# Down projections cut in half between the gate and up groups of a gated feed-forward

## The chip, the core and the metric

The kernel runs on one core of one Trainium2 chip. The metric is the device time of one execution in microseconds (us). Five engines of the core work side by side, each through its own queue in order: TensorE (PE: matmuls; PEld are its weight loads), VectorE (DVE), ScalarE (ACT), GpSimd (POOL) and SyncE (SP, which here issues DMAs only).

## The reference

Two decoder layers over 512 tokens of width 1024 in float32, each a mixer and then a gated feed-forward with a causal convolution of width 3 on its gate. Only the feed-forward is touched by the change:

```
def gated_conv_ffn(x, w_gate, w_up, conv_w, conv_b, w_down):
    g = jnp.einsum('bsd,df->bsf', x, w_gate)          # 1024 -> 2816
    g = causal_dwconv3(g, conv_w) + conv_b
    up = jnp.einsum('bsd,df->bsf', x, w_up)
    return jnp.einsum('bsf,fd->bsd', jax.nn.silu(g) * up, w_down)   # 2816 -> 1024

for layer in range(2):
    h = h + mixer(rms_norm(h, norm_mix[layer]))
    h = h + gated_conv_ffn(rms_norm(h, norm_ffn[layer]), ...)
return rms_norm(h, final_norm)
```

## The kernel before

**Precision by parts.** Every operand of a matmul is held as two tiles, a rounded part (`hi`) and the remainder (`lo`), and every product is three matmuls: hi by hi, hi by lo, lo by hi (`mm3`, L152). So each weight tile and each activation tile needs one ScalarE copy (the `hi`) and one VectorE subtraction (the `lo`). `parts` (L145) does this for weights, `split` (L257) for activations. `summed` (L136) makes the `lo` in another way: ScalarE writes the negated weight, and an accumulating DMA that POOL issues adds the weight to it.

**Groups.** The 2816 hidden channels are 22 rows of 128 (`NF`). `Ffn.hidden(f)` (L757) makes rows f and f+1, gate and up: a group. Groups 0 and 2 use plain matmuls (`direct`, L592). Groups 4 to 20 use `both` (L681), a fast scheme of block products: seven products each for gate and up, 14 in all, each of four inner blocks by three matmuls of 256 columns. They run in the order g1 u1 g5 g6 u5 u6 g2 g7 u2 u7 g4 g3 u4 u3. For their weights VectorE first forms sums of blocks (`s12`, `s34`), and ScalarE and VectorE split those. The names in the profile are `whi_a11`, `whi_s12g`, `wlo_g` and so on for gate, with u for up, and `g_8a` or `u_8b` for the PSUM banks.

**After the products.** ScalarE and VectorE bring the products together out of PSUM into `rows` (gate) and `kept` (up), run the convolution (`c`, `conv`, L561: one ScalarE and two VectorE steps), the silu (`s`, L570) and the product with up. Then `act` (L575) splits the two rows into the four buffers of `acts` (`a_hi`, `a_lo`), and the second buffer pair of a group is the last to be ready.

**Down parts.** `PARTS` (L516) says which rows of the down projection stand behind which groups: rows 0 and 1 behind groups 0 and 2, rows 2 to 5 behind group 4, rows 6 to 9 behind groups 6 and 8, and so on by four; the last part (18 to 21) stands behind groups 18 and 20:

```
PARTS = (((0, 2), 0, 2), ((4,), 2, 6), ((6, 8), 6, 10), ((10, 12), 10, 14),
         ((14, 16), 14, 18), ((18, 20), 18, 22))
for groups, a, b in PARTS:
    for f in groups:
        ffn.hidden(f)
    ...
    project(f"d0_{a}", w_ffn_down[0], ffn.acts, list(range(a, b)), nxt)
```

Part (6, 10) therefore uses rows of both groups before it, one of which has just ended. With four `acts` buffers, the rows of the next group can be split only as these are read for the last time.

In layer 0 a part is a call of `project` (L286), with 1024 output columns in two halves of 512; one half is four PSUM banks, and VectorE adds each to the residual `h`. In layer 1 the tokens are the rows of the output instead (`lhs` is the activation, `rhs` the weight), and a part is a call of `down` (L1145) with eight pieces of 128 tokens by 512 columns that are added to `y`. Its weights are fetched a row of 128 by 1024 at a time. The last part of layer 1 also does the final norm, for which `fin`, the gain, is fetched into one of the staging tiles.

**What is shared.** Weights are fetched by SP into four staging tiles (`raw`, L129) and split into six pairs of buffers (`whi`, `wlo`, L138 and L146). Groups and down parts draw on the same staging tiles, buffers and the seven PSUM banks of `ps_mm`. A scheduler sets the order of the instructions on each engine from the program order and its own account of the times; where the program says `inorder` or `behind`, it is bound to that.

Of the kernel before, what the change touches and what calls it, by code (L numbers as in the profile page):

```python
# [20 lines left out]
FF = 2816  # L21
NF = FF // P
# [10 lines left out]
def tile_trunk(ctx: ExitStack, tc: tile.TileContext, x, norm_mix, norm_ffn, final_norm,  # L33
# [3 lines left out]
    nc = tc.nc  # L37
# [4 lines left out]
    wp = ctx.enter_context(tc.tile_pool(name="wp", bufs=1))  # L42
# [26 lines left out]
    small = cp.tile([P, LINE], F32, name="small")  # L69
# [20 lines left out]
    eps = small[:, 1:2]  # L90
# [42 lines left out]
    def weights(src, a, b, name):  # L133
        return parts(*fetch(src, a, b, name))
# [54 lines left out]
    class Norm:  # L189
# [93 lines left out]
        turn[0] += 1  # L283
        return padded[turn[0] % NPADDED]

    def project(name, w, acts, ks, norm, before=None):  # L286

        for gi in range(2):
            c0 = gi * 512
            chunks = {}  # L290
            for i in range(0, len(ks), 2):
                k0 = min(ks[i], ks[i + 1])
                hi, lo = weights(
                    w[k0 * P : (k0 + 2) * P, c0 : c0 + 512].rearrange("(k p) c -> p k c", p=P),
                    2, 512, f"{name}_{gi}_{k0}")
                chunks[k0], chunks[k0 + 1] = (hi, lo, 0), (hi, lo, 1)
# [12 lines left out]
            group(f"{name}{gi}", range(4), ks, lhs, lambda k, j: acts[k], 4, done,  # L309
                  before if gi == 0 else None)  # L310
# [37 lines left out]
    def mixer0():  # L348
        nonlocal prm0
        w = w_in_even[0]  # L350
        with tc.tile_pool(name="m0", bufs=1) as mp:
# [152 lines left out]
            def b_done(j, ps):  # L504
# [8 lines left out]

    PARTS = (((0, 2), 0, 2), ((4,), 2, 6), ((6, 8), 6, 10), ((10, 12), 10, 14),  # L516
             ((14, 16), 14, 18), ((18, 20), 18, 22))
    HALF = S // 2
    NP = NK // 2
    PAIRS = [k for i in range(NP) for k in (i, i + NP)]  # L520
# [25 lines left out]
    class Ffn:  # L546
# [45 lines left out]
        def direct(self, f, normed, sets, ch, before=lambda i, j: None):  # L592

            layer = self.layer
            banks = {}
            for js in sets:
                for i, k in enumerate(PAIRS):
                    for j in js:
                        before(i, j)
                        hi, lo = ch["gu"[j // 2], i // 4]  # L600
                        c = slice((j % 2) * P, (j % 2 + 1) * P)
                        if j not in banks:
                            banks[j] = mm_bank(f"gu{layer}_{f}_{j}")
                        mm3(banks[j], (hi[:, i % 4, c], lo[:, i % 4, c]), hg_k(k),
                            i == 0, i == NK - 1)

            def evacuate():
                r = self.r
                gates = []
                for j in range(2):  # L610
                    t = padded_tile()
                    if normed:
                        nc.scalar.copy(t[:, 2:], banks[j])
                    else:
                        nc.vector.tensor_tensor(t[:, 2:], banks[j], r, ALU.mult)
                    s = self.silu(self.conv(t, f + j), f + j)
                    if not normed:
                        nc.gpsimd.tensor_tensor(s, s, r, ALU.mult)
                    gates.append(s)
                for j, s in enumerate(gates):  # L620
                    nc.vector.tensor_tensor(s, banks[2 + j], s, ALU.mult)
                    self.act(f + j, s)

            return evacuate

# [55 lines left out]
        def both(self, f):  # L681

            layer, ap, n = self.layer, self.ap, f"{self.layer}_{f}"
# [6 lines left out]
            w = self.unit(f"a11_{n}")  # L690
# [3 lines left out]
            for key in "gu":  # L694
# [6 lines left out]
                w = self.unit(f"s12{key}_{n}")  # L701
# [18 lines left out]
            lo, hi = slice(2, 2 + HALF), slice(2 + HALF, 2 + S)  # L720
# [4 lines left out]
            s, pending = {}, {}  # L725
# [23 lines left out]
                    s[0] = self.silu(self.conv(pads[0], f), f)  # L749
            nc.vector.tensor_tensor(s[1][:, HALF:], kept[:, 2, :], s[1][:, HALF:], ALU.mult)  # L750
            nc.vector.tensor_tensor(s[1][:, :HALF], pending["u", 4], s[1][:, :HALF], ALU.mult)  # L751
            self.act(f + 1, s[1])
            s0 = s[0].rearrange("p (a b) -> p a b", a=2)
            nc.vector.tensor_tensor(s0, kept[:, :2, :], s0, ALU.mult)
            self.act(f, s[0])

        def hidden(self, f, before=lambda i, j: None):  # L757
            if f == 0:
                def first(i, j):
                    before(i, j)  # L760
# [10 lines left out]
                rest()  # L771
            elif f == 2:
                self.direct(2, True, ((0, 1), (2, 3)), self.ch)()
            else:
                self.both(f)

    def ffn0(norm):
        nonlocal prm1
        with tc.tile_pool(name="f0", bufs=1) as ap:
            def sums(kp):  # L780
                return [ap.tile([P, 2, HALF], F32R, name=f"t23{i}_{kp}") for i in "hl"]

            ffn = Ffn(0, prm0, norm, ap, sums)
            nxt = None
            for groups, a, b in PARTS:
                for f in groups:
                    ffn.hidden(f)
                if b == NF:
                    prm1 = params1()
                    nxt = Norm("m1", lambda k: prm1("mix", k))  # L790
                project(f"d0_{a}", w_ffn_down[0], ffn.acts, list(range(a, b)), nxt)
            return nxt


# [264 lines left out]
    def ffn1(norm):  # L1059
        with tc.tile_pool(name="f1", bufs=1) as ap:  # L1060
# [4 lines left out]
            ffn = Ffn(1, prm1, norm, ap, sums)  # L1065
            acts = ffn.acts
# [11 lines left out]
                if i < 2:  # L1078
                    turn_residual(j, i)

            for groups, a, b in PARTS:
                for f in groups:
                    ffn.hidden(f, before=before)
                last = b == NF
                if last:
                    fin = wp.tile([P, D], F32, tag="raw", bufs=4, name="fin")
                    nc.scalar.dma_start(
                        fin, final_norm.rearrange("(o d) -> o d", o=1).to_broadcast([P, D]))
                    root = small[:, 2:3]
                    nc.scalar.activation(root, eps, AF.Sqrt)  # L1090
# [15 lines left out]
                def done(piece, ps):  # L1106
                    t, c0, c1 = piece
                    dst = y[t][:, c0:c1]
                    nc.vector.tensor_tensor(dst, ps, dst, ALU.add)  # L1109
                    if not last:  # L1110
                        return
# [29 lines left out]
                if last:  # L1141
                    pieces[-1:] = [(NT - 1, 512, 768), (NT - 1, 768, D)]
# [45 lines left out]
```

## Time and profile before

| | |
|---|---|
| median of 3 runs | 994.29 us (994.14 to 994.36) |
| the profiled execution, its own time | 994.15 us |
| its span in the trace | 992.4 us |
| granted clock of TensorE, mean | 0.998 |
| regular pair of groups with its down part | 62.19 to 62.28 us |
| DMA | 125.07 MB, mean 126 GB/s |

The profile is of one execution, and times in it are counted from the start of its span. A row of the stretches gives length and busy time of each engine; a row of the timeline gives start, duration, engine, source line, operation and tiles, and in brackets how long the engine was idle before it and what ended the wait. A matmul's duration holds its way through the array, which overlaps the next one; the pace is the distance between starts. The chain of work that ended last is followed back from the end through what each piece waited for. Stretches in which TensorE runs from one matmul to the next show idle time of the other engines that costs nothing.

### The profile page before, as it was taken

What the parts mean: (1) busy time and instruction counts of PE and PEld (TensorE: products, weight loads), DVE (VectorE), ACT (ScalarE), POOL (GpSimd) and SP (SyncE); (2) the same over time, 40 slices, a digit from 0 to 9 for tenths busy, and PEclk for the clock granted to TensorE, in tenths of its full rate; (3) what the DMA queues carried; (4) which work ended last, traced back from release to release, by engine and by line L of the source; (5) the groups of instructions that cost most, each with busy time, mean ns of one, the idle gap of its engine ahead of it and who ended that gap; (6) DMA issues with size and microseconds to landing.
All of it is one profiled execution on the core that took longest, in us unless ns stands there. A gap on an engine that the chain in (4) does not pass through costs nothing.

```text
span 992.4 us, 14934 instructions
## 1 busy us (share of the span) xinstructions
PE 982.9 (99%) x5905; PEld 875.6 (88%) x5905; DVE 728.5 (73%) x1104; ACT 536.3 (54%) x806; POOL 105.3 (11%) x121
## 2 busy tenths in 40 slices
PE   9999999999999999999999999999999999999997
PEld 6788888898999989999888988888989899898996
DVE  6897458967785877858988665399668768687676
ACT  5623346744653746537668634675546366363664
POOL 2141031200000000000300001211000010000100
PEclk9999999999999999999999999999999999999999
DMA  7442225544553645536423513435546456464542
GB/s 246 133 146 85 86 88 131 121 148 118 133 147 97 181 121 132 148 98 180 136 87 93 182 54 97 105 91 130 143 101 159 124 125 173 94 163 126 123 112 85
DMA packets 83073, 125.07 MB, mean 126 GB/s; under 512 B 4308, under 2 KB 56252, under 8 KB 83004
## 3 DMA queue, kind: packets, MB, share of 16 engines
q1 hardware_dynamic: 74028, 98.24, 31.4%
q0 software_dynamic: 7056, 23.60, 13.3%
q10 hardware_dynamic: 1920, 2.30, 0.7%
q8 instruction: 46, 0.75, 0.3%
q14 instruction: 23, 0.19, 0.1%
HBM read 98.42 MB, written 2.10 MB: 101 GB/s over the span
## 4 chain that ended last, share of the span: by engine, by line
PE 94%; issue 1%; DVE 1%; DMA 1%; ACT 0%; DVEq 0%; POOLq 0%; ACTq 0%
PE d L154 4%; PE d L153 4%; PE d L155 4%; PE dn L153 4%; PE dn L154 4%; PE dn L155 4%; PE gu L153 3%; PE gu L154 3%; PE gu L155 3%; PE v L153 1%; PE oo L155 1%; PE oo L153 1%; PE v L155 1%; PE oe L155 1%; PE oe L154 1%; PE v L154 1%
## 5 line engine op out<-in xcount | busy, mean ns | idle before, releaser
L153 PE MATMUL dn<-whi_dn,a_hi 128*128 128x512 f32 (+1 forms) x180 | 69.4, 386 | 0.0
L154 PE MATMUL dn<-wlo_dn,a_hi 128*128 128x512 f32 (+1 forms) x180 | 69.3, 385 | 0.0
L154 PE MATMUL d<-a_lo,whi_d 128*128 128x512 f32 x176 | 68.7, 390 | 0.0
L155 PE MATMUL d<-a_hi,wlo_d 128*128 128x512 f32 x176 | 68.5, 389 | 0.0
L155 PE MATMUL dn<-whi_dn,a_lo 128*128 128x512 f32 (+1 forms) x180 | 67.9, 385 | 0.0
L153 PE MATMUL d<-a_hi,whi_d 128*128 128x512 f32 x176 | 66.9, 390 | 0.0
L566 DVE SCALAR_TENSOR_TENSOR c<-rows,prm,c 128x512 f32<-128x512 f32 x88 | 66.4, 766 | 0.0
L141 POOL DMA_DIRECT2D wlo_g<-raw_g x22 | 19.1, 867 | 373.9 <-ACT wlo_g L140 257.9
L1109 DVE TENSOR_TENSOR y<-dn,y 128x512 f32<-128x512 f32 (+1 forms) x49 | 32.5, 674 | 23.3 <-PE dn L155 23.0
L140 ACT ACTIVATE wlo_g<-raw_g 128x1024 fp32r<-128x1024 f32 x22 | 23.2, 1056 | 42.4 <-PE dn L154 42.4
L572 ACT ACTIVATE s<-c,prm 128x512 f32<-128x512 f32 x44 | 31.7, 720 | 20.5 <-DVE c L566 20.4
L679 DVE TENSOR_TENSOR wlo_s34u<-s34u,whi_s34u 128x1024 fp32r<-128x1024 f32 x18 | 22.0, 1225 | 27.9 <-ACT whi_s34u L678 27.9
L155 PEld LDWEIGHTS dn<-whi_dn,a_lo 128*128 128x128 f32 x180 | 33.8, 188 | 7.3 <-DVE a_lo L262 0.2
L678 ACT ACTIVATE whi_s12u<-s12u 128x1024 fp32r<-128x1024 f32 x18 | 18.9, 1051 | 39.3 <-PE d L154 33.7
L153 PEld LDWEIGHTS dn<-whi_dn,a_hi 128*128 128x128 f32 x180 | 33.8, 188 | 7.0 <-ACT a_hi L260 0.2
L154 PEld LDWEIGHTS dn<-wlo_dn,a_hi 128*128 128x128 f32 x180 | 33.8, 188 | 6.4
L154 PEld LDWEIGHTS d<-a_lo,whi_d 128*128 128x128 f32 x176 | 33.1, 188 | 7.3 <-DVE a_lo L262 0.2
L305 DVE TENSOR_TENSOR h<-d,h 128x512 f32<-128x512 f32 x48 | 32.5, 683 | 9.2 <-PE d L155 9.2
L153 PEld LDWEIGHTS d<-a_hi,whi_d 128*128 128x128 f32 x176 | 32.8, 188 | 7.0
L155 PEld LDWEIGHTS d<-a_hi,wlo_d 128*128 128x128 f32 x176 | 33.0, 188 | 6.7
L260 ACT ACTIVATE a_hi<-s 128x512 fp32r<-128x512 f32 x44 | 27.6, 628 | 16.1 <-DVE s L751 7.4
L149 DVE TENSOR_TENSOR wlo_dn<-raw_dn,whi_dn 128x1024 fp32r<-128x1024 f32 x22 | 26.8, 1220 | 11.6 <-ACT whi_dn L148 11.6
(1274 smaller groups left out, 3469.1 us busy)
## 6 DMA issues: line engine op xcount, KB each, us to landing
raw_g<-in_w_ffn_gate_dram SPq DMA_DIRECT2D x36, 512.0 KB, 4.6
raw_u<-in_w_ffn_up_dram SPq DMA_DIRECT2D x36, 512.0 KB, 4.7
wlo_g<-raw_g POOLq DMA_DIRECT2D x22, 512.0 KB, 4.7
raw_d<-in_w_ffn_down_dram SPq DMA_DIRECT2D x22, 512.0 KB, 4.0
raw_dn<-in_w_ffn_down_dram SPq DMA_DIRECT2D x22, 512.0 KB, 4.0
wlo_u<-raw_u POOLq DMA_DIRECT2D x19, 512.0 KB, 4.6
raw_oe<-in_w_out_even_dram SPq DMA_DIRECT2D x8, 512.0 KB, 3.6
raw_g<-in_w_ffn_gate_dram SPq DMA_DIRECT2D x16, 256.0 KB, 2.9
```

Source lines behind the costliest of these rows:

```text
L140: first = nc.scalar.activation(lo, raw, AF.Copy, scale=-1.0)
L141: nc.gpsimd.dma_start(lo, raw, accum_op=ALU.add)
L149: behind(nc.vector.tensor_tensor(lo, raw, hi.bitcast(F32), ALU.subtract), after[0])
L153: nc.tensor.matmul(ps, lhs[0], rhs[0], start=start, stop=False)
L154: nc.tensor.matmul(ps, lhs[0], rhs[1], start=False, stop=False)
L155: nc.tensor.matmul(ps, lhs[1], rhs[0], start=False, stop=stop)
L260: nc.scalar.activation(hi, src, AF.Copy, scale=scale)
L305: nc.vector.tensor_tensor(h[k], ps, h[k], ALU.add)
L566: nc.vector.scalar_tensor_tensor(c, t[:, i : S + i], prm("cf", i * NF + ft), c, op0=ALU.mult, op1=ALU.add)
L572: nc.scalar.activation(s, c, AF.Silu, bias=self.prm("bf", ft))
L679: nc.vector.tensor_tensor(lo, src, hi.bitcast(F32), ALU.subtract)
L1109: nc.vector.tensor_tensor(dst, ps, dst, ALU.add)
```

## The change

The whole part behind each pair of groups becomes two halves of 512 columns, one behind each group. Columns 0 to 511 of part (6, 10) follow group 8, as before; columns 512 to 1023 follow group 10. Parts (2, 6), (10, 14) and (14, 18) go the same way, behind groups 4 and 6, 12 and 14, 16 and 18. Part (0, 2), with both halves behind group 2, and part (18, 22), behind group 20, stay whole. Behind the first group of each pair (6, 10, 14, 18) the splits of its two rows stand after the half, since the buffers are still read there. In layer 1 all parts but the last now go through `group`, with weights in tiles of two rows by 512 columns.

```
+    STEPS = [(0, False, []), (2, False, [(0, 2, 0), (0, 2, 1)]), (4, False, [(2, 6, 0)])]
+    for f in range(6, NF - 2, 4):
+        STEPS += [(f, True, [(f - 4, f, 1)]), (f + 2, False, [(f, f + 4, 0)])]
+    STEPS[-1][2].append((NF - 4, NF, 1))
```

`half_weights` is the loop that `project` had for its weights, for one half; `project` takes the halves it is to do:

```
+    def project(name, w, acts, ks, norm, before=None, halves=(0, 1)):
+        for gi in halves:
+            chunks = half_weights(name, w, ks, gi)
```

`hidden` returns the function that does the splits, in place of doing them:

```
-                    self.act(f + j, s)
+                return [(f + j, s) for j, s in enumerate(gates)]
...
-            self.act(f + 1, s[1])
...
-            self.act(f, s[0])
+            return [(f + 1, s[1]), (f, s[0])]
...
+            def split_acts():
+                for ft, row in rows:
+                    self.act(ft, row)
+            return split_acts
```

The loop of layer 0:

```
-            for groups, a, b in PARTS:
-                for f in groups:
-                    ffn.hidden(f)
...
-                project(f"d0_{a}", w_ffn_down[0], ffn.acts, list(range(a, b)), nxt)
+            for f, late, down_parts in STEPS:
+                acts = ffn.hidden(f)
+                if not late:
+                    acts()
+                for a, b, half in down_parts:
...
+                    project(f"d0_{a}", w_ffn_down[0], ffn.acts, list(range(a, b)), nxt,
+                            halves=(half,))
+                if late:
+                    acts()
```

And of layer 1, where the body of the old loop is kept as `last_down` for the last part:

```
+            def half_down(a, b, half):
+                ks, cs = list(range(a, b)), slice(half * 512, half * 512 + 512)
+                chunks = half_weights(f"dn{a}", w_ffn_down[1], ks, half)
...
+                group(f"dn{a}_{half}", range(NT), ks, lhs, rhs, 4,
+                      lambda t, ps: add(y[t][:, cs], ps, t))
...
+            for f, late, down_parts in STEPS:
+                splits = ffn.hidden(f, before=before)
+                if not late:
+                    splits()
+                if f == NF - 2:
+                    last_down(NF - 4, NF)
+                    break
+                for part in down_parts:
+                    half_down(*part)
+                if late:
+                    splits()
```

More of the change, by code (lines that the diff above doesn't have):

```diff
@@ L284, in padded_tile, with half_weights @@
         return padded[turn[0] % NPADDED]
[L286 to L296, printed above, removed]
+    def half_weights(name, w, ks, gi):
+        chunks = {}
+        for i in range(0, len(ks), 2):
+            k0 = min(ks[i], ks[i + 1])
+            hi, lo = weights(
+                w[k0 * P : (k0 + 2) * P, gi * 512 : gi * 512 + 512]
+                .rearrange("(k p) c -> p k c", p=P), 2, 512, f"{name}_{gi}_{k0}")
+            chunks[k0], chunks[k0 + 1] = (hi, lo, 0), (hi, lo, 1)
+        return chunks
+    def project(name, w, acts, ks, norm, before=None, halves=(0, 1)):
+        for gi in halves:
+            chunks = half_weights(name, w, ks, gi)
             def lhs(k, j):
@@ L512, in mixer0 @@
             return nxt
-    PARTS = (((0, 2), 0, 2), ((4,), 2, 6), ((6, 8), 6, 10), ((10, 12), 10, 14),
-             ((14, 16), 14, 18), ((18, 20), 18, 22))
+    STEPS = [(0, False, []), (2, False, [(0, 2, 0), (0, 2, 1)]), (4, False, [(2, 6, 0)])]
+    for f in range(6, NF - 2, 4):
+        STEPS += [(f, True, [(f - 4, f, 1)]), (f + 2, False, [(f, f + 4, 0)])]
+    STEPS[-1][2].append((NF - 4, NF, 1))
     HALF = S // 2
@@ L770, in hidden @@
                     self.normalize(kp)
-                rest()
+                rows = rest()
             elif f == 2:
-                self.direct(2, True, ((0, 1), (2, 3)), self.ch)()
+                rows = self.direct(2, True, ((0, 1), (2, 3)), self.ch)()
             else:
-                self.both(f)
+                rows = self.both(f)
+            def split_acts():
+                for ft, row in rows:
+                    self.act(ft, row)
+            return split_acts
     def ffn0(norm):
@@ L784, in ffn0 @@
             nxt = None
-            for groups, a, b in PARTS:
-                for f in groups:
-                    ffn.hidden(f)
-                if b == NF:
-                    prm1 = params1()
-                    nxt = Norm("m1", lambda k: prm1("mix", k))
-                project(f"d0_{a}", w_ffn_down[0], ffn.acts, list(range(a, b)), nxt)
+            for f, late, down_parts in STEPS:
[3 more added lines that the diff above has]
+                for a, b, half in down_parts:
+                    if b == NF and half == 0:
+                        prm1 = params1()
+                        nxt = Norm("m1", lambda k: prm1("mix", k))
+                    project(f"d0_{a}", w_ffn_down[0], ffn.acts, list(range(a, b)), nxt,
+                            halves=(half,))
+                if late:
+                    acts()
             return nxt
@@ L1079, in before, with add, lhs, rhs @@
                     turn_residual(j, i)
[L1081 to L1090, printed above, removed]
+            def add(dst, ps, t):
+                nc.vector.tensor_tensor(dst, ps, dst, ALU.add)
+            def half_down(a, b, half):
+                ks, cs = list(range(a, b)), slice(half * 512, half * 512 + 512)
+                chunks = half_weights(f"dn{a}", w_ffn_down[1], ks, half)
+                def lhs(k, t):
+                    ts_ = slice(t * P, (t + 1) * P)
+                    return acts[k][0][:, ts_], acts[k][1][:, ts_]
+                def rhs(k, t):
+                    hi, lo, n = chunks[k]
+                    return hi[:, n, :], lo[:, n, :]
+                group(f"dn{a}_{half}", range(NT), ks, lhs, rhs, 4,
+                      lambda t, ps: add(y[t][:, cs], ps, t))
+            def last_down(a, b):
+                fin = wp.tile([P, D], F32, tag="raw", bufs=4, name="fin")
+                nc.scalar.dma_start(
+                    fin, final_norm.rearrange("(o d) -> o d", o=1).to_broadcast([P, D]))
+                root = small[:, 2:3]
+                nc.scalar.activation(root, eps, AF.Sqrt)
                 ch = {}
@@ L1108, in done @@
                     dst = y[t][:, c0:c1]
-                    nc.vector.tensor_tensor(dst, ps, dst, ALU.add)
-                    if not last:
-                        return
+                    add(dst, ps, t)
                     sq = tp.tile([P, S], F32, tag="sq", name=f"sqf{t}_{c0}")[:, : c1 - c0]
@@ L1140, in ffn1 @@
                 pieces = [(t, c, c + 512) for t in range(NT) for c in (0, 512)]
-                if last:
-                    pieces[-1:] = [(NT - 1, 512, 768), (NT - 1, 768, D)]
+                pieces[-1:] = [(NT - 1, 512, 768), (NT - 1, 768, D)]
                 down(f"dn{a}", list(range(a, b)), pieces, lhs, rhs, done)
+            for f, late, down_parts in STEPS:
[9 more added lines that the diff above has]
+                    splits()
     def down(name, ks, pieces, lhs, rhs, on_done):
```

## The prediction

> **What bounds the kernel now.** The page comes first: shares of busy time, and the chain that ended last.
>
> ```profile
> span 992.4 us, 14934 instructions
> PE 982.9 (99%) x5905; PEld 875.6 (88%) x5905; DVE 728.5 (73%) x1104; ACT 536.3 (54%) x806; POOL 105.3 (11%) x121
> ...
> PE 94%; issue 1%; DVE 1%; DMA 1%; ACT 0%; DVEq 0%; POOLq 0%; ACTq 0%
> ```
>
> TensorE (PE) is busy in 99% of the span, and the chain is PE's own work for 94%. A change that moves work without removing any can then win only PE's pauses. Next, the busy times by stretch show where those are: one pair of groups with its down part (14 and 16 of layer 0, cut into second group, part, next group), a whole pair, and the end.
>
> ```profile
> 326.47:346.60 20.13, 20.13 (x169) 20.10 (x169) 15.39 (x24) 14.34 (x24) 0.86 (x1) 1.00 0.63 176
> 346.60:368.40 21.80, 21.80 (x98) 17.89 (x98) 18.02 (x29) 7.94 (x10) 0.86 (x1) 1.00 0.51 141
> ...
> 388.67:450.87 62.20, 62.20 (x434) 58.27 (x434) 46.09 (x71) 33.65 (x51) 3.44 (x4) 1.00 0.51 136
> 942.24:963.36 21.12, 20.31 (x169) 20.06 (x168) 15.34 (x24) 14.17 (x23) 0.86 (x1) 1.00 0.51 137
> 985.70:992.40 6.70, 0.00 (x0) 0.00 (x0) 2.16 (x9) 1.30 (x4) 0.00 (x0) 0.68 0.20 78
> ```
>
> Columns: stretch, length, busy time of PE, PEld, VectorE (DVE), ScalarE (ACT) and POOL, granted clock, DMA share, GB/s. In the regular part PE is never idle, and DVE has room in both kinds of stretch (15.4 of 20.1, 18.0 of 21.8). One stretch differs: the last group of layer 1 takes 21.12 us, 0.81 of it idle.
>
> PE's starts give the pace. 256-column matmuls follow each other at 0.12 us, 512-column ones at 0.227. A group is 14 products of 12 matmuls, 14 x 1.44 = 20.16; a part of four rows is 96 x 0.227 = 21.76; a pair with its part 62.08. The six regular pairs take 62.19 to 62.28, so each loses 0.11 to 0.20. PE's rows show where:
>
> ```profile
> 271.17 0.28 PE L535 MATMUL u_8e<-t,wlo_s12u 128*128 128x256 f32 x1
> 271.28 0.37 PE L535 MATMUL u_8a<-t23h,whi_s12u 128*128 128x256 f32 x1
> 271.49 0.28 PE L535 MATMUL u_8a<-t23l,whi_s12u 128*128 128x256 f32 x1
> ...
> 953.77 0.28 PE L535 MATMUL g_20a<-t,wlo_s34g 128*128 128x256 f32 x1
> 954.86 0.39 PE L535 MATMUL u_20b<-hgh,wlo_u 128*128 128x256 f32 x1 [0.81 <-DMA wlo_u<-raw_u]
> 955.08 0.28 PE L535 MATMUL u_20b<-hgh,whi_u 128*128 128x256 f32 x1
> ```
>
> The step from 271.28 to 271.49 is 0.21 in place of 0.12: u's sixth product goes into the bank that ScalarE's copy of u's first product has only just emptied. The step from 953.77 to 954.86 is 1.09: the last group's second u weights arrive late. ScalarE and POOL say why:
>
> ```profile
> 944.23 1.05 ACT L678 ACTIVATE whi_s12u<-s12u 128x1024 fp32r<-128x1024 f32 x1
> 945.18 0.71 ACT L572 ACTIVATE s<-c,prm 128x512 f32<-128x512 f32 x1
> 945.79 0.62 ACT L260 ACTIVATE a_hi<-s 128x512 fp32r<-128x512 f32 x1
> ...
> 947.53 1.04 ACT L140 ACTIVATE wlo_u<-raw_u 128x1024 fp32r<-128x1024 f32 x1
> ...
> 948.88 0.86 POOL L141 DMA_DIRECT2D wlo_u<-raw_u  x1 [8.48 <-ACT wlo_u L140]
> ```
>
> The buffer for wlo_u was free from 942.24, the end of group 18, but ScalarE had silus and splits of group 18 to do ahead of it, and the transfer after it takes 5.94 us in the chain. Both pauses belong to a group that directly follows another.
>
> **What the change removes.** No instruction: the built orders of the two kernels hold equal counts on PE, DVE, ACT, POOL and SP. Only the order differs, and outside the feed-forward layers not even that.
>
> The second groups of pairs (8, 12, 16, 20) now follow a half part of 10.88 us (48 x 0.227). Traced from the end of that half as zero: ScalarE does the deferred splits (0.63 each), the split of s12u (1.05) and then wlo_u at about 0.2 to 0.9; the copy of u's first product ends near 4.3, and its bank is needed at 7.2. wlo_u lands at latest at 0.9 + 1.04 + 0.3 + 5.94 = 8.2 and is needed at 8 x 1.44 = 11.5. So both kinds of pause go: seven of 0.09 (four in layer 0, three in layer 1) are 0.62; the late weights are 0.97, with 0.10 in the slow matmul behind them and 0.10 in a like one at 946.7. Sum 1.79.
>
> **What it costs.** Layer 1's down weights are fetched in 2 KB rows in place of 4 KB: 512 KB land in a median 4.0 us for both (raw_d and raw_dn), so nothing. The deferred splits (two of ACT at 0.63, two of DVE at 0.68) are not needed for 20 us after their half: nothing, unless wlo_u behind them uses up its 3.3 us of cover. The half of columns 512 to 1023, behind the first group of the next pair, reads four tiles that are at least one group old: no wait. The last part, the final norm and the 6.7 us tail stay as they are.
>
> The cost that the trace does not show lies in the halves (2,6), (6,10), (10,14) and (14,18) of columns 0 to 511, eight in both layers, which need fresh splits as the whole parts did. In before, PE has 23 matmuls on old tiles there, until 23 x 0.227 = 5.21 after the group; its second a_hi is done 5.05 after (413.15 + 0.63, where the part's first matmul starts at 408.73), and a_lo 6.20 after (414.25 + 0.68) against 28 matmuls, 6.35. A cushion of 0.15. In the changed order PE has 24 and 29 matmuls ahead (5.44, 6.57), but DVE's queue holds, ahead of the splits, sums of the next group that were behind them before. I work it through from the start of the group as zero, with starts spaced as in DVE's rows (0.60 for 512 columns, 0.33 for 256, 0.66 for a convolution tap, 1.13 for 1024). The first down tile gets its buffer after the fourth product, 5.92 with the matmul's tail; its ACT and DVE halves end at 8.2; that frees a staging tile, and the next gate weights land 4.8 later, 13.0. Four sums and two adds follow to 16.11. The up weights wait for the second down tile (buffer free after the sixth product, 8.80; halves done 11.1) and land at 15.9, 0.2 ahead of their turn. Then eight steps of 0.60, four of 0.33, four taps and one of 1.13 are 9.89: the second a_lo starts at 26.00 and is done at 26.68, or 6.52 after the group. On ACT the second silu starts at 21.93, then come 0.61, 0.95, 0.53, 0.95 and a_hi to 25.60, or 5.44. Against 5.44 and 6.57 that is a cushion of 0.0. Bounds: the fetch of raw_u takes
>
> ```profile
> DMA to landing us min/median/max: 4.8/4.8/5.1
> ```
>
> so a late one, 0.3 over the median with 0.2 to spare, delays by 0.1; twice the cushion of before (0.3) is my upper end, and nothing the lower one (a gain here is excluded, as before does not pause there). I take 0.05, by the working: 8 x 0.05 = 0.4, with bounds 0 and 2.4.
>
> Sum: 994.15 (profiled execution; span 992.4 and 1.75 around it) - 1.79 + 0.4 = 992.8. The median of the runs, 994.29, is 0.14 higher: **992.9**, with its own bounds 992.5 and 994.9.
>
> **Rivals.** Faster by more: every pause in the two feed-forwards goes. Those are 0.85 over the six regular pairs (above 62.08 each), 0.96 in the last group and about 0.58 in the last part: 2.4, hence 991.9. For it: an even load on DVE. Against: the last part is untouched, and the fresh-split halves keep their timing. In the Trainium skill, "Perfetto Trace Analysis" (section Optimization Strategy) advises interleaving regimes whose most contended engine differs, and calls a gap that repeats a sign of missing buffers. The repeating 0.09 us gap bears that out, but PE is the fullest engine in both regimes here (20.13 of 20.13, 21.80 of 21.80), so by this trace the advice is worth these pauses and no more. Chance 0.08.
>
> No effect: the pauses return elsewhere, since ACT, DVE and the transfers do the same work in the same 62 us; 994.3. Against it stands the slack of 3.3 us for wlo_u. Chance 0.15.
>
> Slower: the next group's sums make the splits late in the eight halves. DVE's queue is in order, so a fetch that lands x after its turn at 16.11 moves everything behind it, and PE waits 8 x x. At 5.5 us, as raw_v takes on the page, up weights land at 16.6, x = 0.5, each half waits 0.55 to 0.6: 4.6 more, less 1.79: 997.1. It decides from 0.47 us per half, where 8 x 0.47 - 1.79 reaches 2. Against it: raw_u took 5.1 at most in the regular stretch. Chance 0.12.
>
> Slower by the clock: a pause long enough drops PE's clock. The trace has 1.00 over the pause of 0.81 and 0.68 over the last 6.70 us without a matmul, so the limit lies between. Eight waits of that kind, say 3 us each, would give 994.3 + 24 = 1018 and more. Nothing in the working comes near; chance 0.01. In the Trainium skill, "TensorE: Matmul & The Clock Gate" (section HAM oscillation) puts the limit near 3.4 us of idle PE, which speaks against any schedule that makes PE wait once per part; the trace's 1.00 after 0.81 us agrees as far as it goes.
>
> **The numbers.** The forecast has 0.64. About 0.2%, 2.0 us, is what a measurement of this kernel can tell from no change; forecast and no effect lie within it: same 0.79, faster 0.08, slower 0.13. The range 992.0 to 995.4 takes in the bounds of the fresh-split cost and part of the faster case; it leaves out the slower cases and half of the faster one, 0.17.
>
> **What would show it.** Right: u_20b starts without a DMA wait; a pair with its two halves takes 62.1 to 62.3; no step of 0.21 at u's sixth product. Wrong: PE waits on a_hi or a_lo in a half of columns 0 to 511; idle time of DVE before s12u that ends with a raw_u transfer; PE time in any group above 20.3.

## The result, and the profile after

The changed kernel takes 996.21 us (median of 12 runs, 994.84 to 997.43) against 994.34 for the kernel before (12 runs, 994.03 to 994.51): a ratio of 1.0019, 95% interval 1.0010 to 1.0028. The runs lie 2.6 us apart where those of before lie 0.5 apart. In a second measurement, later and beside other kernels (below, "The changed kernel again"), it was 995.34 against 994.47, 1.0008 (0.9999 to 1.0017). The forecast was 992.9, with a range up to 995.4.

The first lines of the page of the profiled execution (996.58 us) are the span, the busy times and the shares of the chain of waits:

```profile
span 994.9 us, 14982 instructions
PE 984.0 (99%) x5905; PEld 875.8 (88%) x5905; DVE 730.6 (73%) x1104; ACT 538.4 (54%) x806; POOL 105.3 (11%) x121
...
PE 87%; DVE 3%; issue 3%; DMA 2%; ACT 1%; POOL 0%; SPq 0%; DVEq 0%; POOLq 0%; ACTq 0%
```

No engine has more instructions than before (PE, DVE and ACT are busy 1 to 2 us longer), but the chain is PE's own for 87% in place of 94%: it now leaves PE several times, through transfers, VectorE and ScalarE. The waits of PE name the place (what waited, on what; total us, times, longest):

```profile
PE dn L153 <- ACT a_hi L260: 1.3, 2, 0.7
PE clock L62 <- DVE idle L57: 1.3, 1, 1.3
PE d L153 <- ACT a_hi L260: 1.0, 1, 1.0
```

The line of `clock` is the start of the program, as before. The other two are new: down products `d` (layer 0) and `dn` (layer 1) that wait for `a_hi`, the split of the acts. The busy times by stretch (columns as in the prediction) show where there is a wait and where there is none:

```profile
390.48:452.64 62.16, 62.16 (x433) 58.32 (x432) 46.47 (x71) 33.68 (x51) 3.44 (x4) 1.00 0.53 139
757.21:820.30 63.09, 62.43 (x433) 58.22 (x432) 46.41 (x70) 33.91 (x51) 3.41 (x4) 1.00 0.52 134
777.36:789.24 11.88, 11.22 (x50) 8.90 (x49) 11.42 (x18) 6.31 (x9) 0.85 (x1) 1.00 0.57 148
945.52:965.67 20.15, 20.15 (x169) 20.15 (x168) 10.25 (x14) 10.92 (x18) 0.86 (x1) 1.00 0.31 80
```

The first row is a pair of groups with its two halves in layer 0 (from group 16): 62.16 us, PE never idle. The second is a pair in layer 1 (from group 8): 63.09, 0.93 longer. The third is the half of columns 0 to 511 in that pair, and it holds that loss: 11.88 in place of 48 x 0.227 = 10.88. The last row is the last group of layer 1: 20.15, where before it took 21.12. So the gains came, and a larger cost came with them.

The chain of waits around that half (start, duration, what) tells the whole path:

```profile
764.13 1.24 DVE wlo_dn L149
...
765.38 5.30 DMA raw_g<-in_w_ffn_gate_dram
...
770.77 0.69 DVE s12g L706
...
779.24 0.67 DVE c L574
...
781.51 0.61 ACT a_hi L260
782.13 0.95 ACT whi_g L142
783.08 0.53 ACT a_hi L260
783.60 0.04 issue
783.65 0.50 PE dn L153
```

The split of the first down tile (`wlo_dn`) frees a staging tile; the fetch of the next gate weights (`raw_g`) goes into it and takes 5.30 us; VectorE's sum `s12g` waits for it; behind that sum stand, in VectorE's queue, everything up to the last convolution tap, then the silu, `a_hi`, and PE. VectorE's rows show the same wait here, and its absence in the half behind group 16 of layer 1, which does not pause:

```profile
769.33 0.42 DVE L747 TENSOR_TENSOR rows<-g_8e,rows 128x256 f32<-128x256 f32 x1 [0.76 <-ACT rows L737]
770.77 0.69 DVE L706 TENSOR_TENSOR s12g<-raw_g,raw_g 128x512 f32<-128x512 f32 x1 [1.02 <-DMA raw_g<-in_w_ffn_gate_dram]
...
895.49 0.42 DVE L747 TENSOR_TENSOR rows<-g_16e,rows 128x256 f32<-128x256 f32 x1 [0.76 <-ACT rows L737]
895.96 0.69 DVE L706 TENSOR_TENSOR s12g<-raw_g,raw_g 128x512 f32<-128x512 f32 x1
```

From the start of the group (757.21 and 883.37) `s12g` starts at +13.57 in the first and +12.59 in the second; the fetch was issued at +8.18 in both. Over the eight halves with fresh splits (those of columns 0 to 511) `s12g` starts at +12.46 to +13.95, and the four that start after +12.75 pause PE by 1.48, 0.32, 0.99 and 0.97 us. The other four lose 0.06 us or less.

The account of the 2.3 us by which PE's last matmul ends later (987.87, before 985.56): the feed-forwards give back 1.77 of pauses, those four halves cost 3.7, and 0.37 is in the first 200 us, whose order the change does not touch. The end, without PE, is 0.2 longer.

### The profile page after: what moved, and what is told of

Read it like the earlier page. It is cut to its first block, busy times and chain, and to the rows that moved or that the text cites. A ratio compares the mean times of both kernels' runs of the same rounds, so it can differ in the third digit from the quotient of the medians.

```text
span 994.9 us, 14982 instructions
## 1 busy us (share of the span) xinstructions
PE 984.0 (99%) x5905; PEld 875.8 (88%) x5905; DVE 730.6 (73%) x1104; ACT 538.4 (54%) x806; POOL 105.3 (11%) x121
## 4 chain that ended last, share of the span: by engine, by line
PE 87%; DVE 3%; issue 3%; DMA 2%; ACT 1%; POOL 0%; SPq 0%; DVEq 0%; POOLq 0%; ACTq 0%
PE d L153 4%; PE d L154 4%; PE d L155 4%; PE dn L153 3%; PE dn L155 3%; PE dn L154 3%; PE gu L153 3%; PE gu L155 3%; PE gu L154 3%; PE v L153 1%; PE oo L155 1%; PE v L155 1%; PE oo L154 1%; PE v L154 1%; PE oo L153 1%
## 5 line engine op out<-in xcount | busy, mean ns | idle before, releaser
L149 DVE TENSOR_TENSOR wlo_d<-raw_d,whi_d 128x1024 fp32r<-128x1024 f32 x22 | 26.8, 1223 | 31.7 <-ACT whi_d L148 31.7
L140 ACT ACTIVATE wlo_u<-raw_u 128x1024 fp32r<-128x1024 f32 x19 | 20.0, 1054 | 36.7 <-PE d L155 21.3
L148 ACT ACTIVATE whi_d<-raw_d 128x1024 fp32r<-128x1024 f32 x22 | 23.2, 1057 | 29.4 <-issue 3.4
L148 ACT ACTIVATE whi_dn<-raw_dn 128x1024 fp32r<-128x1024 f32 x22 | 23.3, 1057 | 29.0 <-issue 3.0
```

The lines of the kernel that those rows point to most:

```text
L140: first = nc.scalar.activation(lo, raw, AF.Copy, scale=-1.0)
L148: behind(nc.scalar.activation(hi, raw, AF.Copy), after[1])
L149: behind(nc.vector.tensor_tensor(lo, raw, hi.bitcast(F32), ALU.subtract), after[0])
```

## The experiments

Theory 1: the splits of the halves of columns 0 to 511 stand in VectorE's in-order queue behind the next group's sums, these wait for the `raw_g` fetch, and that fetch lands early or late from run to run. Theory 2: ScalarE's order does it (the copies `wlo_g` and `whi_g` ahead of `a_hi`). Theory 3: interleaving in itself costs, or one layer's way of fetching does.

### The changed kernel again

No edit.

> The changed kernel once more, on the chip of the three above. Theory 1: the landing time of eight fetches decides, so runs lie 1.5 to 3 us apart, around 995.5 to 996.5; in this profile the halves that pause need not be those of the first profile (the pauses there were 1.48, 0.26, 0.93 and 0.90 us), and each paused half has its first s12g more than 12.8 us after the start of its group, each half without a pause less. Theories 2 and 3: the same halves pause as before, by the same amounts.

995.34 us (11 runs, 994.68 to 996.34), a little below what I expected. In its profiled run (994.68) the pauses are 1.03, 0.11, 0.77 and 0.14 us; the half behind group 12 of layer 1, which lost 0.97 in the first profile, loses nothing (its `s12g` starts at +12.60; in the first profile at +13.54, its fetch having been issued 0.54 later). This profile is of the fastest of the 11 runs; by the medians the cost against the forecast gains of 1.79 is 2.7 here and 3.7 in the first measurement. The same program pauses in other places in another run, which a fixed cost of interleaving would not. Two halves are late in both: behind group 4 of layer 0 and group 8 of layer 1.

### Gate sums that do not wait for the second fetch

```diff
-                r0, r1 = raws[key, 0][0], raws[key, 1][0]
+                r0, r1 = raws[key, 0][0], raws[key, int(key == "u" or f == 4 or f % 4 == 0)][0]
```

> The changed kernel, in the order that it has on every engine, instruction for instruction; but in groups 6, 10, 14 and 18 the gate's sums s12g and s34g read the first half of the gate weights in place of the second as well, so these sums no longer wait for the second raw_g fetch (part of the computation is changed by this: the combined gate weights of those groups are not the reference's). The fetch itself and ScalarE's copies of it stay. Theory 1 (those four sums, waiting for the fetch ahead of the splits in VectorE's queue, are the whole cause): s12g starts at +12.46 in all eight halves, no wait of PE on a_hi or a_lo of a half of columns 0 to 511 is over 0.1 us, the runs lie within 0.8 us of each other, and the time is 992.4 to 993.2, the forecast of the record. Theory 2 (ScalarE's copies wlo_g and whi_g wait for the same fetch ahead of a_hi): waits remain wherever the fetch is late, 994 to 995.5. Theory 3 (interleaving in itself): 994.7 to 996.3 as the changed kernel.

993.37 us (11 runs, 992.95 to 995.61) against 994.52, 0.9993 (0.9984 to 1.0002): 2.0 below the changed kernel as each stands to the kernel before, and 0.2 above the expected range; its runs are further apart than expected, ten of them within 1.5 us. This kernel leaves the second half of the gate weights out of those sums, so its gate values for these groups are not the reference's. The instructions and their order are the same on every engine; only the wait is gone. The interval against the kernel before still holds 1; against the changed kernel, ten of the eleven runs lie below its fastest. VectorE's rows at the place shown above:

```profile
767.61 0.42 DVE L747 TENSOR_TENSOR rows<-g_8e,rows 128x256 f32<-128x256 f32 x1 [0.75 <-ACT rows L737]
767.95 0.68 DVE L706 TENSOR_TENSOR s12g<-raw_g 128x512 f32<-128x512 f32 x1
```

`s12g` starts at +12.46 in all eight halves, and seven of them lose under 0.08 us. The eighth, behind group 4 of layer 0, still loses 0.33, in steps of 0.11 at most, and its row says why:

```profile
218.02 0.69 DVE L706 TENSOR_TENSOR s12u<-raw_u,raw_u 128x512 f32<-128x512 f32 x1 [0.28 <-DMA raw_u<-in_w_ffn_up_dram]
```

That is the `raw_u` wait which the prediction named; it comes once and costs a third of a microsecond. (In the changed kernel itself `s12u` follows `s12g` at 3.2 us in all eight halves of both profiles, so there it never waits for `raw_u`.) ScalarE's copies still read the second fetch, so theory 2 has no part in these waits: what has to be taken away is VectorE's wait, and with it nearly all of the cost goes.

### ScalarE's copies behind the splits

```diff
-                hi, lo = summed(*raws[key, 1])
+                hi, lo = summed(*raws[key, 1],
+                                after=last["hi"] if f > 4 and f % 4 == 2 else None)
```

(`after` orders `summed`'s first copy; `last["hi"]` is the last `a_hi`.)

> The changed kernel, with only ScalarE's first copy of gate (wlo_g) of groups 6, 10, 14 and 18 ordered behind the last a_hi of the group before; VectorE's queue as in the changed kernel. Theory 1: VectorE still runs the sums ahead of the taps, a late fetch still moves s and the splits; a_hi gains at most about 0.64 us (what the copies took of the 0.82 us pause in the half at 783), so a paused half keeps a rest, and waits of PE on a_hi or a_lo of 0.2 to 0.6 us remain where the fetch lands later than 4.8 us: 993.5 to 995, with a spread over 1 us. Theory 2 (ScalarE's order alone): all waits go and the time is 992.6 to 993.2. Theory 3: 995.5 to 996.5.

995.53 us (11 runs, 995.06 to 997.98), 1.0014 (1.0005 to 1.0023): no gain at all, half a microsecond above what theory 1 gave. ScalarE's rows of the same half:

```profile
780.17 0.64 ACT L263 ACTIVATE a_hi<-s 128x512 fp32r<-128x512 f32 x1
781.84 0.63 ACT L263 ACTIVATE a_hi<-s 128x512 fp32r<-128x512 f32 x1 [1.04 <-DVE s L765]
782.38 1.04 ACT L140 ACTIVATE wlo_g<-raw_g 128x1024 fp32r<-128x1024 f32 x1
```

With the copies away, the second `a_hi` waits 1.04 us for VectorE's `s`. It does end 0.6 us earlier in its half (at +4.57 where the fetch is in time, +5.19 before), but the order built for PE uses the split earlier by as much: after 21 matmuls of the half in place of 24. So a wait of 0.70 stays here, where the changed kernel had 0.61 to 0.82. Theory 2 falls; and a gain for one engine was spent by the built order of another, which theory 1's number had left out.

### The sums behind the splits

```diff
+            fresh = last["lo"] if f > 4 and f % 4 == 2 else None
...
-                       self.added[key])
+                       fresh or self.added[key])
```

(The same for `s34`; `last["lo"]` is the last `a_lo` of the group before.)

> The changed kernel, with one ordering added: VectorE's first sums of the weights of groups 6, 10, 14 and 18 (s12g, s34g, s12u, s34u) go behind the last a_lo of the group before them, so the fresh splits no longer queue behind sums that wait for the raw_g fetch. Theory 1 (a late raw_g fetch, through VectorE's in-order queue, delays the splits of the halves of columns 0 to 511): PE waits on a_hi or a_lo in none of the eight halves, the 3.4 us of the profiled run go, the runs lie within 0.6 us of each other, and the time is 992.6 to 993.2. Theory 2 (ScalarE's order, the copies wlo_g and whi_g ahead of a_hi, makes the splits late): those copies depend on the sums and move as well, so the waits go here too; the next kernel tells these two apart. Theory 3 (the interleaving itself costs, through transfers that collide): the time stays at 995.5 to 996.5 and the runs stay 2 to 3 us apart.

999.25 us (5 runs, 997.93 to 1001.07), 1.0049 (1.0037 to 1.0062): a miss by 6 us, and the slowest kernel of all. PE's waits:

```profile
PE u_6e L545 <- DVE kept L750: 0.9, 1, 0.9
PE u_10e L545 <- DVE kept L750: 0.8, 1, 0.8
...
PE u_6b L545 <- DMA wlo_u<-raw_u: 0.3, 1, 0.3
```

No line names `a_hi`, but two things took its place. The half uses the splits after 15 matmuls, and each of the eight halves loses 0.3 us in short steps. And sums that run late hold their staging tiles longer, so the next fetches go out late, three of them at once: in group 6 of layer 1 SP issues `raw_u` at 738.08, `raw_g` at 738.57 and `raw_u` at 739.40 (732.28, 734.32 and 737.20 in the changed kernel). VectorE then waits for the fetch one group further on:

```profile
743.53 0.69 DVE L709 TENSOR_TENSOR s12g<-raw_g,raw_g 128x512 f32<-128x512 f32 x1 [5.18 <-DMA raw_g<-in_w_ffn_gate_dram]
...
745.67 0.41 DVE L750 TENSOR_TENSOR kept<-u_6e,kept 128x256 f32<-128x256 f32 x1
```

and the bank that `kept`'s add frees is late for u_6e. The wait was moved, not removed.

### One layer at a time

The parts of the other layer go back to whole ones (layer 1's in two calls of half the columns):

```diff
+    WHOLE = [(f, False, [(a, b, h) for h in range(2)] if f == groups[-1] else [])
+             for groups, a, b in PARTS for f in groups]
...
-            for f, late, down_parts in STEPS:
+            for f, late, down_parts in WHOLE:
```

Layer 0 alone in half parts:

> Half parts in layer 0 alone; layer 1 goes back to a whole part behind each pair of groups (issued as two halves one after the other, its weights in the 2 KB rows of the changed kernel). Theory 1: layer 0 brings its four bank pauses (0.36 us) and pays for its four halves with fresh splits, about 1.7 us on average: 995.2 to 996.2, that is slower than before by about 1.3. If the cost sits in layer 1 (its 2 KB rows or its own order of work): 993.8 to 994.2.

Layer 1 alone in half parts:

> Half parts in layer 1 alone; layer 0 goes back to whole parts. Theory 1: layer 1 brings the late weights of the last group and three bank pauses (0.97 + 0.20 + 0.27 = 1.4 us) and pays about 1.7 us on average for its four halves: 994.2 to 995.2, with the spread about half that of the changed kernel's variance. If the cost sits in layer 1: 996 or more; if it sits in layer 0: 992.8 to 993.1.

Layer 0 alone: 994.86 us against 994.17 (11 runs, 994.15 to 996.19), 1.0005 (0.9995 to 1.0014). Layer 1 alone: 993.84 (993.13 to 994.84), 0.9994 (0.9985 to 1.0003). Both intervals hold 1. The medians stand at +0.7 and -0.3 where theory 1 gave about +1.3 and +0.3: each is lower than I expected, and the times alone decide nothing here. Layer 0 has little to gain (0.36) and the half behind group 4, late in every profile; layer 1 has the late weights of its last group to gain. The profile of layer 0 alone lost 1.66 and 0.52 us in two halves, that of layer 1 alone 0.52 in one. Both profiles show the cost, so it is not layer 1's rows of 2 KB.

### Splits used as late as the half allows

On top of "ScalarE's copies behind the splits", the half takes its old rows first for all four banks, then its fresh rows in the order in which they are split:

```diff
+    def part_rows(a, b, half):
+        fresh = half == 0 and 0 < a < NF - 4
+        return [a, a + 1, a + 3, a + 2] if fresh else list(range(a, b))
...
-            group(f"{name}{gi}", range(4), ks, lhs, lambda k, j: acts[k], 4, done,
+            group(f"{name}{gi}", range(4), ks, lhs, lambda k, j: acts[k],
+                  2 if ks[2:] and ks[2] > ks[3] else 4, done,
```

> copies_behind showed that the order built for PE took back what ScalarE gained: the fresh rows were used 21 matmuls after the start of the half in place of 24. Here PE's half takes all 24 matmuls of the old rows first, then row f+1, then row f, in the order in which VectorE and ScalarE split them; ScalarE's copies stay behind a_hi. By the times of copies_behind the splits of a fetch in time end at +2.9 and +4.57 (a_hi) and +4.51 and +5.71 (a_lo) after the start of the half, and are needed at +5.44, +6.12, +5.90 and +6.57: 0.86 us of cover. Theory 1: a fetch is covered up to an s12g at +13.3, so of the pauses seen only those of the latest fetches stay (13.6 to 14.2: 0.3 to 0.9 us in the half behind group 4 of layer 0), PE waits 0.3 to 1 us in all, and the time is 992.8 to 993.8, below the changed kernel by 1.5 or more. Theory 3: 994.7 to 996.3.

993.53 us (11 runs, 993.14 to 994.25), 0.9992 (0.9983 to 1.0000): within the expected range, 1.9 below the changed kernel as each stands to the kernel before, and the runs lie 1.1 us apart. Six halves lose 0.02; `s12g` starts at +13.43 behind group 8 of layer 1, which now costs 0.25, and at +13.79 behind group 4 of layer 0, which costs 0.81. A cover of some 0.9 us swallows most of the late fetches, as theory 1 says.

### The part cut by rows

In place of half the columns of four rows, all columns of the two rows that are a group old; no fresh split is needed and none is deferred.

```diff
-    STEPS = [(0, False, []), (2, False, [(0, 2, 0), (0, 2, 1)]), (4, False, [(2, 6, 0)])]
-    for f in range(6, NF - 2, 4):
-        STEPS += [(f, True, [(f - 4, f, 1)]), (f + 2, False, [(f, f + 4, 0)])]
-    STEPS[-1][2].append((NF - 4, NF, 1))
+    STEPS = [(0, False, []), (2, False, [(0, 2, 0), (0, 2, 1)])]
+    STEPS += [(f, False, [(f - 2, f, 0), (f - 2, f, 1)]) for f in range(4, NF - 2, 2)]
+    STEPS += [(NF - 2, False, [(NF - 4, NF, 0), (NF - 4, NF, 1)])]
```

> The part cut by rows in place of columns: behind each group f from 4 to 18 both column halves of rows f-2 and f-1, which are a whole group old; splits not deferred; the last part (18 to 22) whole as before. The same matmuls on PE; VectorE adds twice as often into h and y (16 in place of 8 adds per four rows, 8 x 0.6 us = 5 us more of VectorE per 62 us, of which it has some 16 idle). Theory 1: no matmul needs a split of the group just done, so a late raw_g fetch has the whole half part to be caught up in; no waits on a_hi or a_lo outside the last part, the gains of 1.8 us stay, 992.3 to 993.2, spread under 0.6 us. Theory 3 (interleaving halves costs by itself): 995 or more, with a spread like the changed kernel's. If the adds delay the sums: waits of PE on whi or wlo of the next group, 994 to 996.

995.15 us (11 runs, 994.17 to 997.64), 1.0006 (0.9996 to 1.0015): slower than theory 1 had it, and within the 994 to 996 that was named for adds that delay the sums. No wait on `a_hi`, as theory 1 says, but a new one ahead of groups, in the profiled run (997.64) mostly in layer 0:

```profile
PE g_8a L542 <- ACT rows L736: 1.3, 1, 1.3
...
PE g_10a L542 <- ACT rows L736: 0.6, 1, 0.6
```

ScalarE's rows there:

```profile
269.56 1.06 ACT L685 ACTIVATE whi_s34u<-s34u 128x1024 fp32r<-128x1024 f32 x1 [2.40 <-DVE s34u L714]
270.52 0.35 ACT L736 COPY rows<-g_8a 128x256 f32<-128x256 f32 x1
```

The copy that empties the bank of the group's first product stands behind the split of `s34u`, and that waits for VectorE, which has the additional adds to do and is itself late where the fetch is. In layer 1 of that run it did not happen, so two versions followed.

### Layer 1 cut by rows, layer 0 as before

The `STEPS` of the cut by rows for layer 1, the `WHOLE` of above for layer 0.

> A version that might beat both: layer 0 with whole parts as before, layer 1 cut by rows as in rows_cut, where the profile had no wait of PE in layer 1 outside the last part except 0.2 us. Layer 1 brings the late weights of the last group and three bank pauses (1.4 us) and pays at most the 0.2 us: 992.8 to 993.4, faster than before by 0.9 to 1.5, with a spread like that of before. If rows_cut's layer 1 was a lucky profile: 994 or more.

994.65 us (11 runs, 993.41 to 995.54), 1.0002 (0.9993 to 1.0011): no gain. Its profile has the wait of the copies in layer 1 now, 0.87 ahead of g_12a and 0.69 ahead of g_14a. The quiet layer 1 of the run before was luck.

### The cut by rows, with one split moved

```diff
-                w = self.unit(f"s34{key}_{n}")
-                self.halves(*w, s34)
-                put(key, 7, w, 0)
-                put(key, 3, w, 1)
+                def split34(key=key, s34=s34):
+                    w = self.unit(f"s34{key}_{n}")
+                    self.halves(*w, s34)
+                    put(key, 7, w, 0)
+                    put(key, 3, w, 1)
+
+                if key == "g":
+                    split34()
...
+                if (key, product) == ("g", 5):
+                    split34()
```

> rows_cut with one instruction of ScalarE and its VectorE partner moved: the split whi_s34u is issued behind the copies of the group's first products (rows, kept) in place of ahead of them. In rows_cut the first bank of layer 0's groups came free late because ScalarE's copy stood behind whi_s34u, which waited for VectorE's s34u (1.43 us at 269.38, 0.72 at 301.97, 0.44 to 0.57 at three more). If that queue order is the reason: those waits go, 992.4 to 993.4, below rows_cut by 1.5 to 2.5. If the bank is late for another reason: 995 as rows_cut.

992.56 us (11 runs, 991.83 to 995.78) against 994.52, 0.9988 (0.9979 to 0.9996): the version that beats both kernels. The waits ahead of the groups are gone. Eight of the runs lie between 991.83 and 992.70, the other three at 994.20 to 995.78. The profiled one is among these three, and VectorE's rows and PE's name its loss:

```profile
891.56 0.42 DVE L750 TENSOR_TENSOR rows<-g_16e,rows 128x256 f32<-128x256 f32 x1 [0.70 <-ACT rows L740]
896.19 0.69 DVE L705 TENSOR_TENSOR s12g<-raw_g,raw_g 128x512 f32<-128x512 f32 x1 [4.20 <-DMA raw_g<-in_w_ffn_gate_dram]
...
899.06 0.42 DVE L750 TENSOR_TENSOR kept<-u_16e,kept 128x256 f32<-128x256 f32 x1
```

```profile
899.53 0.39 PE L542 MATMUL u_16e<-hgh,whi_s34u 128*128 128x256 f32 x1 [1.22 <-DVE kept L750]
```

It is the same fetch in front of the same queue, taking about 6 us; here `s12g` has to start some 3 us late before PE notices. But it was also issued late, at 890.05, which is +10.61 in its group in place of +8.18, between two fetches of `raw_u` (889.59 and 890.60). This lateness was handed on from group to group: in layer 1 `s12g` starts at +14.34, +15.08, +15.76 and +16.74 behind groups 10, 12, 14 and 16. What SP waited for ahead of the three fetches was POOL's accumulating transfer `wlo_u<-raw_u`, which reads a staging tile; it released SP at +10.01 of the group, and at +5.95 in the same group of the changed kernel. A fifth staging tile, which might let the fetch go out earlier, was not tried.

## Why the prediction was wrong

**What bounds the kernel.** Right. Nothing but PE's pauses changed; PE's matmuls and their pace are the same.

**The gains.** Right in kind and size. Forecast 1.79 (0.62 in the bank pauses, 1.17 at the last group); the feed-forwards outside the fresh halves lose 1.77 less. u_20b starts without a wait, the last group takes 20.15, and a pair without a late fetch takes 62.16.

**Deferred splits, 2 KB rows, halves of columns 512 to 1023.** Costed at nothing, and no wait of PE names any of them, though the median landing of `raw_dn` went from 4.0 to 4.9 us with the 2 KB rows.

**The fresh-split halves.** This is the step that failed, as a mis-sized term: "I take 0.05, by the working: 8 x 0.05 = 0.4, with bounds 0 and 2.4". Measured: 3.7 in the first profile and 2.0 in the second. The path itself was worked out rightly, first down tile, staging tile, fetch, sums, splits, and for a fetch in time its steps hold within 0.6 us (fetch issued at 8.2 in both; `s12g` forecast at 13.0, measured at 12.46). The cushion of 0.0 came out near: a fetch in time leaves 0.28, since PE pauses from `s12g` at +12.74. That is partly luck, as two errors of opposite sign met: `s12g` in time starts 0.54 earlier than forecast, and from its start to the end of the second `a_hi` the trace takes 12.88 us (from +12.46 to 5.19 after the group) where the working has 12.60. Two things were wrong.

First, the bound was taken from the wrong transfer. The text says that `raw_u` lands "0.2 ahead of their turn" and bounds the delay by its row of 4.8/4.8/5.1. That row is also misread: it holds three transfers with a known landing, of which two are POOL's accumulating ones (`wlo_u<-raw_u`, 4.8 each), and the one fetch among them took 5.1. And `raw_g`, which the text lets land 4.8 after the issue, without a spread, stands ahead on the same path with almost no slack behind it, although its landings do spread in the trace of before. For the groups of layer 0, and then of layer 1, the answer for `raw_g` there reads:

```profile
DMA to landing us min/median/max: 3.7/4.6/5.8
```

```profile
DMA to landing us min/median/max: 3.7/4.6/6.2
```

These rows mix in POOL's transfers too; of SP's fetches, the landing is known for eight: 3.7 to 5.0 us in layer 0 and 3.7 to 6.2 in layer 1. A landing at 6.2 in place of the 4.8 of the working, through a cushion of 0.0, gives a pause of 1.4: the longest gaps of the late halves reach 1.2 and 1.4.

Second, a wait is one-sided. With no cushion, an early fetch gains nothing and a late one costs its whole delay, so the term is the mean of max(0, delay) over the fetches and not the delay of a median one. In the 24 halves of the four profiles with this order, the longest gap is `s12g`'s start less 12.74 us wherever that is positive by more than 0.2 (0.28 for 13.02, 0.61 for 13.35, 0.82 for 13.57, 1.21 for 13.95, 1.42 for 14.16). A paused half loses 0.16 to 0.28 us more than its longest gap, as the matmuls behind the gap are slower too. Eight such terms, one a half, make the cost; that their scatter makes most of the spread of the runs fits the two profiles and is not shown beyond them. The kernel before has the same fetches and hides them: there the sums came behind the splits, and its second `a_hi` ends 5.06 after the group in all eight places. VectorE's rows of before, where the part behind group 16 of layer 0 starts at 408.73:

```profile
414.25 0.68 DVE L262 TENSOR_TENSOR a_lo<-s,a_hi 128x512 fp32r<-128x512 f32 x1
414.85 0.68 DVE L698 TENSOR_TENSOR s12g<-raw_g,raw_g 128x512 f32<-128x512 f32 x1
```

**The rivals.** "Slower: the next group's sums make the splits late" had the queue and the direction, a price (0.55 to 0.6 us per half) and a chance of 0.12; the transfer that it named, and its evidence against, "raw_u took 5.1 at most", were about `raw_u`, where the runs show `raw_g`. The rival of the clock did not come: the granted clock in the halves with a pause is 1.00. In the Trainium skill, "TensorE: Matmul & The Clock Gate" (section HAM oscillation) puts the limit near 3.4 us of idle PE; the longest gap in this profile, 1.2 us, agrees as far as it goes. The Trainium skill's "Perfetto Trace Analysis" (section Optimization Strategy) reads a repeating gap as a possible sign of missing buffers; the new gap agrees with that, since its fetch starts at 765.38, as soon as `wlo_dn` (764.13, 1.24) has freed the tile.

## What to carry to other kernels

When a change puts an in-order queue's wait for a transfer ahead of work that PE needs, cost it by the spread of that transfer's landing, from its own row, through the cushion that is left: with none, every late landing is lost and no early one is gained. Before moving such work, count what stands between the transfer and PE on every queue; moving one engine's instructions alone lets the built order of another spend the gain, as two of these kernels did. Cut a part so that it needs only operands that are a whole stage old, and then look for the next queue in which something late stands ahead of something needed.

## What the hardware showed that was not expected

The consumer of one fetch of 512 KB, at the same place of the same program, moved by 0.9 us from run to run (`s12g` at +13.54 and at +12.60 behind group 12 of layer 1); 0.54 of that was a later issue, the rest a later landing. Part of the lateness goes with what was issued just before. Over 40 halves in six profiles of kernels with column halves, where the `raw_u` ahead of it was issued 7.6 us or more after the start of the group, that is at most 0.6 ahead of `raw_g`, `s12g` started at +12.83 to +14.16 (7 of 7); where `raw_u` was out at 6.4 or earlier, it started by +12.63 in 21 of 25. The other four are all behind group 8 of layer 1, at +13.35 to +13.57. The eight in between (`raw_u` at 6.6 to 6.9) started at +12.60 to +13.08.

The packets in the kept traces hold a candidate for the places that are always late, which no run tested. Behind group 8 of layer 1, in the four late cases, a packet of 16 KB of the instruction queue (q8) begins at +10.35 to +11.20 and takes 0.9 to 1.0 us; fifteen of the sixteen packets of 4 bytes that close the fetch end by +11.81, and the last at +12.25 to +12.97. Such a packet also begins at +7.83 to +8.00 behind group 4 of layer 0, in five of the seven cases above, so that there the two cannot be told apart. Against it stands the profile of layer 1 alone: its packet at that place begins at +11.07, and `s12g` starts at +12.46. Whether the packet delays the fetch only where both use the same DMA engine, the traces do not tell.
